# Hybrid encoder trunk: activations kept as [channels, tokens] from the first stage to the output

## Chip, cores and metric

One core of one Trainium2 chip. The metric is the device time of one launch in microseconds: the kernel before took 3477.07 us (median of 3 runs, 3474.01 to 3480.54).

## What is computed

Two groups of tokens (2048 and 256, together T = 2304) pass through two layers with shared weights, D = 1024. Every float32 operand of a large product is held as two parts, hi and lo, in TensorE's one-pass format (fp32r), and a product is three matmuls (`mm3`).

```python
# layer 0
h = x + concat(gqa(rms(x)), diff_attention(rms(x))) @ w_out_ab      # 8 rotary heads, 4 differential heads
h = h + sigmoid(rms(h) @ w_ple_gate[0]) * (p[0] @ w_ple_proj[0])
# layer 1
u, g = split(rms(h) @ w_in_c)                                       # pooling mixer
h = h + ((pooled(u) - u) @ w_grp * scale * silu(g)) @ w_out_c
h = h + sigmoid(rms(h) @ w_ple_gate[1]) * (p[1] @ w_ple_proj[1])
```

## The kernel before

The program is one stream per engine, ordered by hand and by a scheduler. Its stages, with the place that each has in the profiled span:

1. **Stage 1** (0 to 295 us). For each of the 9 blocks of 256 tokens: x comes in as rows, two tiles of [128 tokens, 1024]; `norm_rows` (L181) takes the sum of squares on ACT, rsqrt and the scaling by row on POOL; `transpose_rows` (L189) turns each tile by 8 PE transposes (L195) into channels on the partitions and splits it from PSUM with ACT (hi, L117) and DVE (lo, L118). Then the rotary heads' projections. The split x also goes to DRAM (`xT_d`).
2. **Attention A and B with fillers** (295 to about 2350 us). `drive` interleaves the heads' steps with filler steps: `proj_b`, then `proj_out(0)`, `proj_ple(0)`, `fold_c`, `proj_ple(1)`, `proj_out(512)`. `proj_out` (L738) takes 128 tokens at a time: the activations (yh, yl) stand still and 512 columns of the weights move, 12 matmuls into one bank; DVE adds the residual (L756), which is loaded and stored as rows of `h_d`. `proj_ple` (L759) turns its input by two PE transposes (L768).
3. **Drain of proj_out(512)** and loading of the gate's weights (to 2424 us): 6 of the 8 weight chunks are loaded before, 2 after the drain.
4. **Gate of layer 0** (to 2631 us), 18 tiles of 128 tokens: `gate_half` (L875) twice a tile, 24 matmuls each with 512 weight columns moving (po, then pf), sigmoid on ACT (L883), product and sum on DVE (L884, L885); `turned` (L896) turns the next tile's normalised rows, 8 transposes among them.
5. **Pooling mixer** (to 3058 us), 9 blocks: here the weights stand still and 256 tokens move. The next block's x is turned (16 transposes) while the groups are multiplied.
6. **`out_ple`** (L945, to 3464 us), 18 tiles of 128 tokens: output projection of layer 1 (pa, weights moving, 48 matmuls of 512), norm, 8 transposes, gate (48 matmuls of 512), sum, store.

In stages 1, 4, 5 and 6 the rows that ACT and DVE split are read from PSUM. All DMAs go through SP's queue.

```python
def transpose_rows(xn, hi, lo, col):                      # L189
    for half in range(2):
        pt = pt_()
        for j in range(4):
            pe.transpose(pt[:, j * P : (j + 1) * P], xn[:, ...], ident)
        split_ps(pt..., hi[:, cs, col : col + P], lo[:, cs, col : col + P])
```

Of the kernel before, what the change touches and what calls it, by code (L numbers as in the profile page):

```python
# [33 lines left out]
WG_A = 6  # L34
# [5 lines left out]
def trunk_kernel(ctx: ExitStack, tc: tile.TileContext, ins, outs):  # L40
# [4 lines left out]
    pin = [ins["p_prompt"][:, 0], ins["p_sample"][:, 0]]  # L45
    yout = [outs[0][0], outs[1][0]]
# [24 lines left out]
    # activations between the stages; "h" and "l" are the two parts of a split value  # L71
# [7 lines left out]
    h_d = dscratch("h_d", [T, D])  # L79
    m_d = dscratch("m_d", [D, D])  # L80
    pp_d = [dscratch(f"pp{i}_d", [T, D]) for i in range(2)]

# [16 lines left out]
    # products that warm the array up while the first loads run  # L99
# [5 lines left out]
    def rstd_of(ss, scale, n, extra=None):  # L105
        """(ss * scale + eps) ** -0.5 on [P, n]"""
# [17 lines left out]
    def split_w(st, hi, lo, gain=None):  # L124
        """hi + lo = st (weights by rows) times gain by row"""
# [11 lines left out]
    def load_w(pool, w, rows_, cols, tag, gain=None, stage=None, most=512):  # L137
        """columns [(from, to), ...] of w, chunks of 128 rows: a list of split (hi, lo)"""
# [36 lines left out]
    def mm3(out, lhs, rhs, first, last):  # L175
        """out += (lhs_hi + lhs_lo).T @ (rhs_hi + rhs_lo), less lo * lo"""
# [4 lines left out]
    def norm_rows(pool, xt, nb=2):  # L181
        ss = small.tile([P, 1], F32, tag="ss", name="ss")
        xn = pool.tile([P, D], F32, tag="xn", name="xn", bufs=nb)
        ac.activation(xn, xt, AF.Square, accum_out=ss)  # L184
        r = rstd_of(ss, 1.0 / D, 1)
        po.tensor_scalar(out=xn, in0=xt, scalar1=r, scalar2=1.0, op0=ALU.mult, op1=ALU.mult)
        return xn
# [11 lines left out]
    def load_q(pool, row0, nh, t0, n):  # L199
        """the parts of q, each on both halves of the partitions: two [P, nh, n]"""  # L200
# [13 lines left out]
    # =========================== norm, projections of the rotary heads ===========================  # L214
    with tc.tile_pool(name="p1c", bufs=1, reuse_waits="tile") as p1c, \
# [10 lines left out]
        def chain(t0, xts):  # L226
            xh = p1.tile([P, KC, NB], F32R, tag="xh", name="xh")
            xl = p1.tile([P, KC, NB], F32R, tag="xl", name="xl")
            for tt, xt in enumerate(xts):
                transpose_rows(norm_rows(p1, xt, 1), xh, xl, tt * P)  # L230
            store2(xT_d, (xh, xl), lambda d: d[:, t0 : t0 + NB].rearrange("(c p) t -> p c t", p=P))
# [506 lines left out]
    def proj_out(k0):  # L738
# [3 lines left out]
        for tq in TILES[k0 // 512]:  # L742
            while not ready[k0 // 512][tq // P]:
                yield 0.0
# [388 lines left out]
```

## Time and profile before

| | |
|---|---|
| median of 3 runs | 3477.07 us |
| span of the profiled execution | 3470.0 us |
| the median less that span | 7.07 us |
| TensorE matmul busy | 3408.2 us, 98% of the span |
| weight load, DVE, ACT, POOL busy | 88%, 56%, 48%, 48% |
| chain that ended last | PE 91%, DMA 4%, DVE 2%, ACT 1%, issue 1% |
| DMA | 437.76 MB, mean 126 GB/s |

The last matmul ends at about 3465 us; behind it are a sigmoid, two DVE operations and the last store. A matmul's record is longer than its turn on the array, since matmuls are pipelined: its price is the distance from one start to the next.

### The profile page before, as it was taken

The page shows a single profiled execution, that of the slowest core. Times are in us where ns is not written, and L with a number is a line of the kernel's source. Part 1 is how long each engine was busy: PE and PEld are TensorE (multiplying, and loading weights), DVE is VectorE, ACT ScalarE, POOL GpSimd, SP SyncE. Part 2 cuts the span into 40 slices and gives each one's busy share as a digit, 9 for nine tenths or more (in the row PEclk, how much of TensorE's full clock was granted, in tenths as well). Part 3 has the DMA queues.
Part 4 walks back from the last instruction along what each step waited for, and adds up shares of the span by engine and source line. Part 5 has one row for each costly group of instructions (what it writes and reads, how often), then busy time and mean ns, then how long its engine had stood idle before and what let it go on. Part 6 is the DMA issues. An engine that isn't in the chain of part 4 may idle for free.

```text
span 3470.0 us, 60660 instructions
## 1 busy us (share of the span) xinstructions
PE 3408.2 (98%) x21942; PEld 3043.7 (88%) x21942; DVE 1936.7 (56%) x4314; ACT 1671.8 (48%) x3108; POOL 1662.0 (48%) x2013
## 2 busy tenths in 40 slices
PE   9999999999999999999999899999999999999999
PEld 8998999998899988888888788887889999988887
DVE  4336666677666677658778787763434222342222
ACT  4235666666666666546677676751324111221111
POOL 5664545454645455337777687841113455420000
PEclk9999999999999999999999999999999999999999
DMA  7444323234423224653443525268534122353332
GB/s 250 158 141 135 112 77 109 79 109 125 141 82 98 91 77 127 190 180 108 122 125 114 149 91 149 87 196 267 186 133 157 62 72 70 99 164 115 112 113 73
DMA packets 459635, 437.76 MB, mean 126 GB/s; under 512 B 33992, under 2 KB 400584, under 8 KB 458312
## 3 DMA queue, kind: packets, MB, share of 16 engines
q1 hardware_dynamic: 459336, 433.88, 40.4%
q8 instruction: 174, 2.85, 0.3%
q14 instruction: 125, 1.02, 0.1%
HBM read 269.15 MB, written 164.63 MB: 125 GB/s over the span
## 4 chain that ended last, share of the span: by engine, by line
PE 91%; DMA 4%; DVE 2%; ACT 1%; issue 1%; POOL 0%; SPq 0%; DVEq 0%; ACTq 0%; POOLq 0%
PE pf L177 10%; PE pf L179 10%; PE pf L178 10%; PE pt L339 9%; PE pa L377 6%; PE pa L378 6%; PE po L177 6%; PE po L179 6%; PE po L178 6%; PE pa L178 4%; PE pa L177 4%; PE pa L179 4%; PE po L471 3%; PE po L470 3%; PE pt L195 2%; DMA v<-vl_d 1%
## 5 line engine op out<-in xcount | busy, mean ns | idle before, releaser
L389 ACT ACTIVATE s<-s,mx 128x1024 f32<-128x1024 f32 x512 | 585.6, 1147 | 137.3 <-DVE s L442 63.4
L347 DVE TENSOR_TENSOR pl<-pt,ph 128x512 fp32r<-128x512 f32 x780 | 522.4, 686 | 195.0 <-ACT ph L343 188.1
L343 ACT CAST ph<-pt 128x512 fp32r<-128x512 f32 x780 | 438.7, 584 | 276.3 <-PE pt L339 113.5
L339 PE MATMUL pt<-ident,s 128*128 128x128 f32 x3120 | 465.3, 273 | 4.5 <-DVE pl L347 1.9
L339 PEld LDWEIGHTS pt<-ident,s 128*128 128x128 f32 x3120 | 369.7, 141 | 52.4 <-DVE pl L347 4.6
L109 POOL TENSOR_SCALAR rstd<-ss 128x1 f32<-128x1 f32 x72 | 16.0, 222 | 656.4 <-ACT xn L184 654.8
L623 DVE CUSTOM_DVE_ANT_0 s<-pa,dist,mx 128x512 f32<-128x512 f32 x384 | 286.7, 747 | 70.5 <-PE pa L378 55.8
L643 POOL TENSOR_TENSOR s<-s 128x1024 f32<-128x1024 f32 (+1 forms) x136 | 313.0, 2318 | 0.2
L452 POOL TENSOR_SCALAR s<-s,rs 128x1024 f32<-128x1024 f32 (+1 forms) x272 | 298.6, 1110 | 12.1
L442 DVE TENSOR_SCALAR_CACHE_REDUCE s<-pa,mx 128x512 f32<-128x512 f32 x384 | 286.0, 745 | 23.2 <-PE pa L378 13.9
L470 PE MATMUL po<-ph,vA 128*128 128x256 f32 x1040 | 281.2, 292 | 1.1 <-ACT ph L343 1.1
L471 PE MATMUL po<-pl,vA 128*128 128x256 f32 x1040 | 279.5, 295 | 1.1 <-DVE pl L347 1.1
L177 PE MATMUL pf<-xh,wh 128*128 128x256 f32 x944 | 265.6, 281 | 1.7 <-DMA xh<-xTh_d 1.7
L178 PE MATMUL pf<-xl,wh 128*128 128x256 f32 x944 | 266.3, 282 | 0.5 <-DMA xl<-xTl_d 0.5
L179 PE MATMUL pf<-xh,wl 128*128 128x256 f32 x944 | 265.8, 282 | 0.7 <-DVE wl L131 0.7
L377 PE MATMUL pa<-kk,q 128*128 128x512 f32 (+1 forms) x528 | 220.8, 419 | 12.8 <-DMA kk<-kTl_d 11.5
L377 PE MATMUL pa<-kA,q 128*128 128x512 f32 (+1 forms) x528 | 222.8, 422 | 3.9 <-DVE s L442 3.7
L884 DVE TENSOR_TENSOR sg<-pp,sg 128x512 f32<-128x512 f32 x72 | 50.3, 698 | 285.3 <-ACT sg L883 280.0
L378 PE MATMUL pa<-kA,q 128*128 128x512 f32 (+1 forms) x528 | 207.0, 392 | 0.0
L378 PE MATMUL pa<-kk,q 128*128 128x512 f32 (+1 forms) x528 | 206.9, 392 | 0.0
L470 PEld LDWEIGHTS po<-ph,vA 128*128 128x128 f32 x1040 | 196.8, 189 | 11.3 <-ACT ph L343 1.7
L471 PEld LDWEIGHTS po<-pl,vA 128*128 128x128 f32 x1040 | 196.7, 189 | 7.5 <-DVE pl L347 3.0
(232 smaller groups left out, 9701.0 us busy)
## 6 DMA issues: line engine op xcount, KB each, us to landing
xr<-h_d SPq DMA_DIRECT2D x54, 512.0 KB, 3.3
q<-qTh_d SPq DMA_DIRECT2D x144, 128.0 KB, 2.9
q<-qTl_d SPq DMA_DIRECT2D x144, 128.0 KB, 3.0
xh<-xTh_d SPq DMA_DIRECT2D x18, 1024.0 KB, 5.5
xl<-xTl_d SPq DMA_DIRECT2D x18, 1024.0 KB, 7.9
h_d<-xr SPq DMA_DIRECT2D x72, 256.0 KB, 4.0
pp_d<-xr SPq DMA_DIRECT2D x72, 256.0 KB, 2.1
pp<-pp_d SPq DMA_DIRECT2D x36, 512.0 KB, 3.8
```

Of the source, the lines that this page charges most:

```text
L177: pe.matmul(out, lhsT=lhs[0], rhs=rhs[0], start=first, stop=False)
L178: pe.matmul(out, lhsT=lhs[0], rhs=rhs[1], start=False, stop=False)
L179: pe.matmul(out, lhsT=lhs[1], rhs=rhs[0], start=False, stop=last)
L339: pe.transpose(pt[:, (c * 2 + i) * P : (c * 2 + i + 1) * P], s[:, (c0 + c) * P : (c0 + c + 1) * P], ident)
L343: ac.copy(ph, pt)
L347: ve.tensor_tensor(out=pl, in0=pt, in1=ph.bitcast(F32), op=ALU.subtract)
L377: pe.matmul(ps, lhsT=q1, rhs=k[:, i * 512 : i * 512 + w], start=True, stop=False)
L378: pe.matmul(ps, lhsT=q2, rhs=k[:, i * 512 : i * 512 + w], start=False, stop=True)
L389: ac.activation(s[:, c], s[:, c], AF.Exp, bias=bias, scale=-1.0, accum_out=sums[i])
L470: pe.matmul(ov[0][:, 0:256], lhsT=v, rhs=ph[:, c], start=c0 + c == 0, stop=False)
L471: pe.matmul(ov[0][:, 0:256], lhsT=v, rhs=pl[:, c], start=False, stop=c0 + c == nk - 1)
L643: po.tensor_tensor(out=sc[0][:, k], in0=sc[0][:, k], in1=sc[1][:, k], op=ALU.subtract)
```

## The change

Host side: `xT` [1024, 2304] and `pT` are handed to the kernel beside the rest, and the outputs come back as [1024, tokens].

On the chip:

- The residual lives as `hT_d` [D, T] (two of them), the embedding's projection as `pp_d` [D, T]. A block is 256 tokens with all 1024 channels, tile [128, 8, 256], loaded in pieces of 1 KB.
- Normalising is `scaled`: r of 256 tokens is spread over the partitions by two PE transposes, ACT copies it (L190), and POOL multiplies the block by it in two instructions of 128x1024 (L192; in the mixer DVE does this). `split_sb` then splits in SBUF: ACT casts (L196), DVE subtracts (L197), 1024 columns each, twice.
- The sums of squares need PE too: ACT squares, POOL or DVE adds, and `tok_sums` multiplies by a column of ones (L204, 4 matmuls of one column, float32, per block).
- In the gates, `out_c`, `proj_out` and `proj_ple` weights stand still and 256 tokens move: each matmul of 512 columns becomes two of 256.
- Gate 0 finds r of the next block from a load of h (`r_here`) while it works on this one; the mixer and gate 1 use r kept from sums of the stage before (`r_all`). The gate's last sum moves from DVE to POOL (L1033).
- All 8 chunks of gate 0's weights are loaded before the drain ends, and the first block's chain starts among `proj_out(512)`'s last blocks.
- `proj_out` fetches y and the residual one step ahead; its buffers for the residual go from 4 to 3.
- The last stage is two passes over the blocks: `out_c` for all 9 (h stored), then gate 1.
- In stage 1 the first block is still turned by 16 transposes; the other eight use `scaled`.

```diff
+    def scaled(ht, r, xn, rb, eng=po):
+        pr = pt_()
+        for i in range(2):
+            pe.transpose(pr[:, i * P : (i + 1) * P], r[:, i : i + 1].broadcast_to([P, P]), ident)
+        ac.copy(rb, pr[:, :NB])
+        for cs in HALVES:
+            eng.tensor_tensor(out=xn[:, cs], in0=ht[:, cs], in1=rb.unsqueeze(1).broadcast_to([P, KC // 2, NB]), op=ALU.mult)
+
+    def split_sb(xn, hi, lo):
+        for cs in HALVES:
+            ac.copy(hi[:, cs], xn[:, cs])
+            ve.tensor_tensor(out=lo[:, cs], in0=xn[:, cs], in1=hi[:, cs].bitcast(F32), op=ALU.subtract)
+
+    def tok_sums(sm, n):
+        pst = pt_()
+        for i in range(2):
+            for k in range(n):
+                pe.matmul(pst[:, i : i + 1], lhsT=sm[:, k, i * P : (i + 1) * P], rhs=ones[:, 0:1], start=k == 0, stop=k == n - 1)
+        return pst[:, 0:2]
...
     def proj_out(k0):
...
-                xr = fw.tile([P, 512], F32, tag="xr", name="xr", bufs=4)
+            xr = fw.tile([P, 2, NB], F32, tag="xr", name="xr", bufs=3)
...
-                    mm3(ps, (yh[:, c], yl[:, c]), W[a // 128 + c], c == 0, c == 3)
+                        mm3(ps[:, m * NB : (m + 1) * NB], (w[0][:, ms], w[1][:, ms]), (yh[:, c], yl[:, c]), c == 0, c == 3)
...
+    def product(W, x, j):
+        ps = (po_, pf_)[j % 2]()
+        for m in range(2):
+            ms = slice((j * 2 + m) * P, (j * 2 + m + 1) * P)
+            for c in range(KC):
+                mm3(ps[:, m * NB : (m + 1) * NB], (W[c][0][:, ms], W[c][1][:, ms]), (x[0][:, c], x[1][:, c]), c == 0, c == KC - 1)
+        return ps.rearrange("p (m t) -> p m t", t=NB)
...
+        def chain(t0):
+            ht = h_block(src, t0)
+            xn = pool.tile([P, KC, NB], F32, tag="sq", name="xn", bufs=1)
+            r = yield from r_of(t0, ht, xn)
+            scaled(ht, r, xn, work[0].tile([P, NB], F32, tag="rb", name="rb"))
+            x = parts()
+            split_sb(xn, *x)
+            return ht, x
...
+            for j in range(KC // 2):
+                js = slice(j * 2, j * 2 + 2)
+                ps = product(W, x, j)
+                now, pp = pp, embedded(b * 4 + j + 1)
+                if j == 0 and pend:
+                    pend.pop()()
+                sg = pool.tile([P, 2, NB], F32, tag="sg", name="sg", bufs=2)
+                ac.activation(sg, ps, AF.Sigmoid)
+                ve.tensor_tensor(out=sg, in0=now, in1=sg, op=ALU.mult)
+                po.tensor_tensor(out=ht[:, js], in0=ht[:, js], in1=sg, op=ALU.add)
+                sy.dma_start(dst(t0)[:, js], ht[:, js])
+                if more:
+                    summed(pool, acc, ht[:, js], j)
+                if j < 3:
+                    go()
...
+    def r_here(t0, ht, sq):
+        sm = pw.tile([P, 2, NB], F32, tag="sm", name="sm", bufs=1)
+        for i, cs in enumerate(HALVES):
+            ac.activation(sq[:, cs], ht[:, cs], AF.Square)
+            ve.tensor_reduce(out=sm[:, i], in_=sq[:, cs].rearrange("p c t -> p t c"), axis=AX.X, op=ALU.add)
...
-    WG0 = load_w(pw, wpg[: WG_A * P], WG_A * P, [(0, D)], "wg", gple[0][:, :WG_A])
+    WG0 = load_w(pw, ins["w_ple_gate"][0], D, [(0, D)], "wg", gple[0])
+    while not through:
+        next(fill)
+    chain = gate_chain(pw, hT_d[0], r_here)
+    first = run(chain(0))
     for _ in fill:
         pass
...
-    out_ple("right", ins["w_out_c"][0], 0, ycT_d, 1, lambda t: rows(yout, t, P))
...
+            for j in range(KC // 2):
+                js = slice(j * 2, j * 2 + 2)
+                ve.tensor_tensor(out=ht[:, js], in0=product(WO, y, j), in1=ht[:, js], op=ALU.add)
+                sy.dma_start(chans(hT_d[0], t0)[:, js], ht[:, js])
...
+        gate(pw, WG, 1, nxt, chain, lambda t0: chans(outs[0], t0) if t0 < S0 else chans(outs[1], t0 - S0), None, iter(()))
```

Counted over the program: 3888 matmuls of 512 columns become 7776 of 256 (gates 1728, `out_c` 864, `proj_out` 864, `proj_ple` 432); of the 576 transposes at L195, 16 stay, so 70 groups of 8 go; the 36 pairs at L768 go; 35 pairs of transposes for r and 27 groups of 4 one-column matmuls come.

What the change moves, at two places. First TensorE in gate 0. Before, a tile's last matmuls into po and the next tile's transposes, which are followed by this tile's pf:

```order
L177 MATMUL po<-wh,nh 128x512
L178 MATMUL po<-wl,nh 128x512
L179 MATMUL po<-wh,nl 128x512
L195 MATMUL pt<-ident,xn 128x128 x8
L177 MATMUL pf<-wh,nh 128x512
L178 MATMUL pf<-wl,nh 128x512
```

Now, in the last group (pf) of a block, the two transposes that spread the next block's r (rt):

```order
L175 MATMUL pf<-yh,wh 128x256
L176 MATMUL pf<-yl,wh 128x256
L177 MATMUL pf<-yh,wl 128x256
L189 MATMUL pt<-ident,rt 128x128 x2
L175 MATMUL pf<-yh,wh 128x256
L176 MATMUL pf<-yl,wh 128x256
```

Before, a whole group of 24 matmuls of 512 stood between the transposes and the products that need them; now 30 matmuls of 256 follow the r transposes in every other block, and 46 in the blocks between, before the next block's first product.

Second, POOL in gate 0 (rstd, rt, r_all: the factors r; xn: the normalised tile; ht: the residual; acc: the squares' sum). Before, one tile after the other:

```order
L109 TENSOR_SCALAR rstd<-ss 128x1
L112 TENSOR_TENSOR rstd<-rstd,mhalf 128x1
L186 TENSOR_SCALAR xn<-xr,rstd 128x1024
L109 TENSOR_SCALAR rstd<-ss 128x1
L112 TENSOR_TENSOR rstd<-rstd,mhalf 128x1
```

Now, one block:

```order
L210 TENSOR_TENSOR r_all<-r_all,mhalf 128x2
L1033 TENSOR_TENSOR ht<-ht,sg 128x512
L1054 TENSOR_TENSOR acc<-acc,sq 128x512
L210 TENSOR_TENSOR rt<-rt,mhalf 128x2
L1033 TENSOR_TENSOR ht<-ht,sg 128x512
L192 TENSOR_TENSOR xn<-ht,rb 128x1024 x2
L1054 TENSOR_TENSOR acc<-acc,sq 128x512
```

The scaling was one instruction with one tensor operand for 128 tokens, done long before its turn; it is two instructions with two tensor operands for 256 tokens, between the sums of the block that is being worked on, and it stands behind the r transposes.

## Rows read from the trace of the kernel before

**Rows 1.** The page: busy time of each engine; shares of the chain that ended last

```profile
PE 3408.2 (98%) x21942; PEld 3043.7 (88%) x21942; DVE 1936.7 (56%) x4314; ACT 1671.8 (48%) x3108; POOL 1662.0 (48%) x2013
PE 91%; DMA 4%; DVE 2%; ACT 1%; issue 1%; POOL 0%; SPq 0%; DVEq 0%; ACTq 0%; POOLq 0%
```

**Rows 2.** Timeline of PE (start, duration, line, out<-in, shapes, count), mixer, first and last of 17

```profile
2799.76 0.28 PE L177 MATMUL po<-xh,wh 128*128 128x256 f32 x1
...
2801.64 0.28 PE L178 MATMUL pf<-xl,wh 128*128 128x256 f32 x1
```

**Rows 3.** Timeline of PE, one tile of out_ple

```profile
3199.82 0.40 PE L178 MATMUL pa<-wl,yh 128*128 128x512 f32 x1
3204.96 0.39 PE L179 MATMUL pa<-wh,yl 128*128 128x512 f32 x1
3205.19 1.04 PE L195 MATMUL pt<-ident,xn 128*128 128x128 f32 x8
3205.98 0.48 PE L177 MATMUL pa<-wh,yh 128*128 128x512 f32 x1
3206.30 0.40 PE L178 MATMUL pa<-wl,yh 128*128 128x512 f32 x1
3211.67 0.40 PE L177 MATMUL po<-wh,nh 128*128 128x512 f32 x1
3222.35 0.40 PE L179 MATMUL pf<-wh,nl 128*128 128x512 f32 x1
```

**Rows 4.** Timeline of PE in stage 1, first and last of 19 matmuls

```profile
259.76 0.28 PE L177 MATMUL pf<-xh,wh 128*128 128x256 f32 x1
...
261.92 0.28 PE L177 MATMUL pf<-xh,wh 128*128 128x256 f32 x1
```

**Rows 5.** Groups by line, PE: shapes, count, busy us, mean ns of one, idle before

```profile
L195 PE MATMUL pt<-ident,xn 128*128 128x128 f32 x576 | 76.7, 273 | 2.3 <-POOL xn L186 2.3
L768 PE MATMUL pf<-ident,pl 128*128 128x128 f32 x72 | 14.1, 273 | 0.1
```

**Rows 6.** Timeline of PE, one-column matmuls (each leaves two records)

```profile
2342.77 0.50 PE L673 MATMUL pt<-ones,sq 128*128 128x1 f32 x4
2343.13 0.48 PE L178 MATMUL pa<-wlo,yh 128*128 128x512 f32 x1
2343.45 0.39 PE L179 MATMUL pa<-whi,yl 128*128 128x512 f32 x1
```

**Rows 7.** Timeline of PE, transposes that spread a row's factor

```profile
1906.70 0.38 PE L681 MATMUL pt<-ident,rstd 128*128 128x128 f32 x2
1906.91 1.47 PE L339 MATMUL pt<-ident,s 128*128 128x128 f32 x12
```

**Rows 8.** Lines of ACT, DVE and POOL: instructions nearest to the added ones

```profile
L184 ACT ACTIVATE xn<-xr 128x1024 f32<-128x1024 f32 x50 | 53.5, 1070 | 96.0 <-issue 80.0 <-DVE xr L974 16.1
L885 DVE TENSOR_TENSOR xr<-xr,sg 128x512 f32<-128x512 f32 x72 | 49.6, 689 | 3.0
L643 POOL TENSOR_TENSOR s<-s 128x1024 f32<-128x1024 f32 x128 | 307.2, 2417 | 0.0
```

**Rows 9.** Timeline of POOL, then of DVE, in attention B

```profile
1577.62 4.76 POOL L643 TENSOR_TENSOR s<-s 128x1024 f32<-128x1024 f32 x2
...
1580.74 2.19 DVE L128 TENSOR_TENSOR wlo<-st,whi 128x512 fp32r<-128x512 f32 x1
1584.12 0.68 DVE L128 TENSOR_TENSOR wlo<-st,whi 128x512 fp32r<-128x512 f32 x1
```

**Rows 10.** Timeline of PE: waits in the drain and at gate 0's start

```profile
2337.38 0.47 PE L177 MATMUL pa<-whi,yh 128*128 128x512 f32 x1 [2.32 <-DVE xr L756]
...
2420.63 0.50 PE L177 MATMUL po<-wh,nh 128*128 128x512 f32 x1 [1.90 <-ACT wh L130]
2426.87 0.50 PE L177 MATMUL po<-wh,nh 128*128 128x512 f32 x1 [1.86 <-ACT sg L883]
```

**Rows 11.** Windows, PE, after the first of these waits

```profile
2338.00:2342.00 4.00, 4.00 (x12) 0.60 0.94 320
```

More of the change, by code (lines that the diff above doesn't have):

```diff
@@ new lines, in parts, with gate_chain @@
+    def parts():
+        pool = turn(1)
+        return [pool.tile([P, KC, NB], F32R, tag=t, name=t) for t in ("yh", "yl")]
+    def gate_chain(pool, src, r_of):
+        def chain(t0):
[6 more added lines that the diff above has]
+            return ht, x
+        return chain
@@ new lines, in paired, with go, value, keep_r @@
+    def paired(step):
+        got = []
+        def go():
+            if not got:
+                try:
+                    next(step)
+                except StopIteration as e:
+                    got.append(e.value)
+        def value():
+            while not got:
+                go()
+            return got[0]
+        return go, value
+    def keep_r(pend, acc, t0):
+        pend.append(lambda: rstd_ps(tok_sums(acc, 2), r_all[:, t0 // P : t0 // P + 2]))
+    def gate(pool, W, layer, nxt, chain, dst, more, after):
+        def embedded(n):
+            if n < len(BLOCKS) * 4:
+                pp = pool.tile([P, 2, NB], F32, tag="pp", name="pp", bufs=2)
+                sy.dma_start(pp, chans(pp_d[layer], BLOCKS[n // 4])[:, n % 4 * 2 : n % 4 * 2 + 2])
+                return pp
+        pend, pp = [], embedded(0)
+        for b, t0 in enumerate(BLOCKS):
+            ht, x = nxt
+            go, value = paired(chain(t0 + NB) if t0 + NB < T else after)
+            go()
+            if more:
+                acc = pool.tile([P, 2, NB], F32, tag="acc", name="acc", bufs=1)
+            for j in range(KC // 2):
+                js = slice(j * 2, j * 2 + 2)
[8 more added lines that the diff above has]
+                sy.dma_start(dst(t0)[:, js], ht[:, js])
+                if more:
+                    summed(pool, acc, ht[:, js], j)
+                if j < 3:
+                    go()
+            nxt = value()
+            if more:
+                keep_r(pend, acc, t0)
+                more(t0)
+        while pend:
+            pend.pop()()
+        return nxt
@@ L946, in trunk_kernel, with mid, chain_c @@
-    transpose_rows(xn, *x0, P)
+    def mid(t0):
+        if t0 == 2 * NB:
+            load_c(wp[0], 0)
+    def chain_c(t0, late=0):
+        ht = h_block(hT_d[1], t0)
+        for _ in range(late):
+            yield
+        scaled(ht, r_all[:, t0 // P : t0 // P + 2], ht, work[0].tile([P, NB], F32, tag="rb", name="rb"), ve)
+        x = parts()
+        split_sb(ht, *x)
+        return x
+    nxt = gate(gx, WG0, 0, first, chain, lambda t0: chans(hT_d[1], t0), mid, chain_c(0, 2))
     for p_ in ple0[::-1]:
@@ L993, in trunk_kernel, with loaded @@
+    def loaded(t0):
+        y = parts()
+        load2(ycT_d, y, lambda d: chans(d, t0))
+        return y, h_block(hT_d[1], t0)
     with pool_ as ws:
```

301 lines of the change are left out of this document (151 added, 150 removed).

## Prediction

> **What bounds the kernel now.** The page comes first: TensorE is busy for 98% of the span, and the chain that ended last is PE for 91% [rows 1]. So the time is the sum of what each matmul takes of the array, plus the moments in which TensorE waits. Busy time is of no use for the first (records overlap), so I read the timelines for the distance from start to start [rows 2 to 4, 6, 7], and for the second the bracketed waits of the same view [rows 10]. The reader is to see how even the starts are: a matmul with 512 moving columns comes every 0.227 us in the gate (47 steps from 3211.67 to 3222.35) and every 0.2336 us in `out_c` (22 steps from 3199.82 to 3204.96) [rows 3]; one with 256 columns comes every 0.1175 us in the mixer (16 steps) [rows 2] and every 0.120 us in stage 1 (18 steps) [rows 4]. Neither half is half of the whole.
>
> **Terms on TensorE.**
> - *512 columns become twice 256.* I take 0.1185 us for 256, between the two rows that I have, since no row tells which of them the new stages resemble. A gate pair then costs 0.237 against 0.227: 1728 x 0.010 = +17. `out_c`: 864 x 0.0034 = +3. The fillers have the gate's shape and I give them 8 ns each: 1296 x 0.008 = +10. Sum +30. By 0.1175 it is 7776 x 0.001 = 8 less, by 0.120 it is 12 more.
> - *Transposes that go.* Eight take 0.79 us (3205.19 to 3205.98), and the matmul behind them takes 0.32 instead of 0.23 [rows 3]: 0.88 a group. 70 of the 72 groups behind the 576 records go [rows 5]: -62. The 36 pairs on the embedding go [rows 5], each 0.21 [rows 7] and some re-entry: -8.
> - *What comes.* 35 pairs for r at the same 0.23: +8. One group of `tok_sums` is four one-column matmuls; two of them (four records) take 0.36, and the next matmul 0.09 more than usual [rows 6]: 0.72 + 0.09 = 0.81, times 27 = +22.
>
> Together 30 - 70 + 30 = **-10 us**, between -18 and +2. The gain from no longer turning is mostly spent on the halves and the sums.
>
> The Trainium skill has another price for the halves: "TensorE: Matmul & The Clock Gate", section "Back-to-back issue gap", gives N columns over 2.4 GHz plus about 2.5 ns. By that estimate two halves cost only 2.5 ns more than the whole, +10 instead of +30. The starts of [rows 2 to 4] do not agree with it, so the sum does not use it.
>
> **Terms in waits.** Before, the next tile's turning was a whole group ahead. Now the next block's chain starts at the r transposes. I price it in gate 0, from the transposes on: the pair 0.3; the copy of 256 columns, a quarter of a 1.07 us ACT row, 0.3 [rows 8]; POOL's two products, 2.42 each by the nearest two-operand row of that size; ACT's cast of 1024 columns, 1.07; DVE's subtraction, two rows of 0.69, 1.3 [rows 8].
>
> The subtraction now reads two tensors in SBUF, where before it read PSUM and SBUF. Beside a busy POOL that means this: a DVE subtraction of two SBUF operands takes 0.68 alone, but 2.19 when it starts at 1580.74 while POOL's second product of a pair runs [rows 9]. POOL ends at 1582.38 and DVE at 1582.93, 0.55 later. It did not slow down, it stood until POOL was through. So the first half's lo cannot be made while POOL makes the second half.
>
> Thus, counted from the transposes: first POOL product to 3.0; cast to 4.2 (hi is there); second POOL product to 5.5; DVE to 6.8 (lo of the first half); cast of the second half to 6.6, DVE to 8.1. TensorE has 30 matmuls to go in half of the blocks (3.9 us with the pair) and 46 in the others (5.8). The next block's first product needs hi at once, lo one matmul later, and the second half 12 matmuls later, 1.4 us. In the short case it waits 6.8 - 3.9 = 2.9, in the long one 1.0. Four blocks of each: **+16 us**. Bounds: if DVE is not held, the second half still ends near 7.9 and the sum is about 10; if a further two-operand DVE instruction of the block (0.69) catches POOL in each half, it is 27.
>
> The other places:
> - *Gate 0's first block.* Its chain has only 24 matmuls of the drain to hide under (2.8 us): some 4 us of waiting. It replaces the waits of 1.90 and 1.86 that stand at the same place now [rows 10]: 0.
> - *Head of stage 1.* The second block's chain, the same 8 us, starts behind ACT's and DVE's splitting of the weights: +4, between 0 and 8.
> - *Start of the mixer.* DVE scales and splits there while it also makes the lo parts of the mixer's weights (two SBUF operands), beside POOL's pooling: +4, between 0 and 8.
> - *`proj_out`.* Fetching ahead would take away waits for the residual like the 2.32 in rows 10, but with three buffers the load of a step waits for the store of three steps earlier: 0, between -5 and +8.
> - *Last stage.* Its chain runs a whole block ahead (192 matmuls, 23 us), its 19 MB more of DMA (h of 2304 x 1024 float32 stored and loaded once more) are spread over 400 us, and the mixer's and gate 1's r is kept: 0. If that cover went, it would cost the 8 us of the chain per block.
> - Fewer instructions on POOL, ACT and DVE in the turned stages: 0, those engines end no chain there.
>
> **Sum.** -10 + 16 + 0 + 4 + 4 + 0 = +14 us. The profiled execution's span of 3470.0 becomes 3484; the median stands 7.07 above that span, so I forecast **3491 us**.
>
> **Rivals.**
> 1. *The chain is covered: faster.* Place: the start of each gate block. It decides whether POOL's two products and what follows end before pf's last matmuls; the point is a chain of about 5.5 us instead of 8.1, that is POOL products of 1.1 us, or a scheduler's 46 matmuls that turn out longer than the chain's first half. Then the 16 us and the two 4s fall away, and the TensorE term stands alone: 3477 - 10 = 3467. For it: POOL's queue has little else in gate 0, and the mixer's turned chain left no waits. Against it: the 2.42 us rows, 128 of them. 0.13.
> 2. *Half of the waits: no change.* The hold of DVE costs less because DVE's queue is in step with POOL, head and mixer cost nothing: -10 + 10 = 0, 3477. 0.20.
> 3. *Cheap halves.* The new matmuls come at 0.1137, half of 0.2275, if a matmul's turn has next to no fixed part, so that two halves cost a whole: the +30 falls to +10 and the forecast to 3471. No row shows such a pace. This is what the Trainium skill's issue gap, cited above, amounts to. 0.05.
> 4. *Slower still.* A wait above two microseconds can also cost the clock: after the wait of 2.32 the granted clock was 0.60 over 4 us, a mix of 1.2 and 2.4 GHz, with 12 matmuls where 17 fit, 1.2 us lost [rows 10, 11]; behind the waits of 1.90 and 1.86 no such loss is seen. Were all four long waits to trip it and POOL be caught by DVE as in the upper bound: 3491 + 11 + 5 = 3507. 0.12.
>
> That the change does not take the turning away is excluded: the transposes are gone from the order.
>
> **How the numbers follow.** The forecast has the remaining 0.50. About 0.2%, 7 us, is what a measurement of this kernel can tell from none, so "faster" is under 3470 and "slower" over 3484. Faster: rival 1 for the most part, and a little of rivals 2 and 3: 0.13. The same: most of rivals 2 and 3, and a little of the forecast's lower end: 0.25. Slower: 0.62. The range leaves out the far halves of rivals 1 and 4: 3467 to 3508. The forecast's own range, from its bounds, is 3480 to 3503.
>
> **What would show it.** Right: no L195 in the mixer and the last stage; starts 0.237 apart per pair in the gates; in gate 0, waits of 1 to 3 us at each block's first product, with DVE's subtraction (L197) as releaser; L197's mean well over 1.3 us there; the stage longer than before, the mixer and stage 1 shorter by 5 to 10 us each. Wrong: no waits at gate 0's blocks; pairs at 0.227; or waits of `out_c` and gate 1 on loads, which I priced at nothing.

## The result, and the profile after

The changed kernel takes 3529.89 us (median of 4 runs, 3529.05 to 3542.31), the kernel before 3476.5 beside it: ratio 1.0161, 95% interval [1.0146, 1.0176]. It is slower, as forecast, but by 53 us and not by 14: outside the range of 3467 to 3508.

The profiled execution of that run was a long one (span 3540.5). The same kernel was profiled again in the first experiment (span 3525.9, run's median 3526.94), and the rows below are of that execution unless another is named. First the page: busy time of TensorE, and the shares of the chain that ended last, to be laid beside [rows 1].

```profile
PE 3425.6 (97%) x25484; PEld 3225.4 (91%) x25484; DVE 2024.4 (57%) x4199; ACT 1684.4 (48%) x3037; POOL 1929.0 (55%) x2042
PE 81%; DMA 6%; DVE 5%; issue 3%; POOL 3%; ACT 1%; SPq 0%; POOLq 0%; DVEq 0%; ACTq 0%
```

The share of TensorE in the chain falls from 91% to 81%; DMA, DVE, POOL and issue, 7% together before, are now 17%. TensorE is busy at almost the same share: the page's first line alone would hide the change.

A table by stage says where. Each border is the start of a matmul in the timeline: the first that reads kA, the last that reads v, the last on the fillers' weights (whi, wlo), the last on gate 0's weights, the last on the mixer's, the last of all. Lengths in us:

| | stage 1 | attention | drain | gate 0 | mixer | last stage | last matmul starts |
|---|---|---|---|---|---|---|---|
| before | 292.2 | 2041.4 | 82.0 | 210.0 | 424.6 | 414.4 | 3464.6 |
| changed | 288.9 | 2049.8 | 90.6 | 259.4 | 413.6 | 417.6 | 3519.9 |
| difference | -3.3 | +8.4 | +8.6 | **+49.4** | -11.0 | +3.2 | +55.3 |
| by the terms of the prediction | -8 | +2 | 0 | +25 | -10 | +5 | +14 |

The mixer and the last stage came as forecast. Nearly all the loss is in gate 0, 6% of the span before. Its waits on TensorE (who waits, who ends the wait, us in total, times, longest), from 2440 to 2700 us:

```profile
PE po L176 <- DVE yl L197: 13.4, 11, 2.4
PE pt L204 <- DVE sm L1060: 6.1, 9, 1.5
PE po L175 <- ACT yh L196: 4.8, 5, 2.1
PE pt L189 <- POOL rt L210: 0.3, 1, 0.3
```

In gate 0 of the kernel before, TensorE waits 3.8 us, the two waits of 1.90 and 1.86 in [rows 10]. The second line is one that the prediction has no word for: the one-column matmuls of `tok_sums` wait for the sums that DVE makes.

Windows of the same stage, of before and then of the changed kernel (length, TensorE busy and matmuls, weight loads, DVE, ACT, POOL, granted clock, DMA share, GB/s):

```profile
2500.00:2550.00 50.00, 50.00 (x242) 41.85 (x241) 15.78 (x25) 13.74 (x26) 7.46 (x12) 1.00 0.42 142
2550.00:2600.00 50.00, 50.00 (x238) 41.77 (x237) 17.73 (x28) 14.55 (x28) 8.41 (x15) 1.00 0.41 137
```

```profile
2440.00:2500.00 60.00, 51.96 (x406) 50.35 (x404) 30.51 (x31) 22.01 (x36) 35.10 (x23) 0.94 0.46 144
2500.00:2550.00 50.00, 44.39 (x345) 42.63 (x346) 21.18 (x18) 14.93 (x22) 32.02 (x20) 0.97 0.31 96
2550.00:2600.00 50.00, 46.03 (x380) 44.87 (x379) 18.35 (x17) 14.91 (x23) 25.98 (x19) 1.00 0.38 117
2600.00:2650.00 50.00, 44.48 (x350) 42.86 (x348) 22.08 (x18) 15.88 (x22) 26.62 (x17) 0.97 0.34 106
2650.00:2700.00 50.00, 47.92 (x371) 47.33 (x372) 18.71 (x24) 18.07 (x30) 26.86 (x19) 0.93 0.42 130
```

Two things are to be seen. TensorE is no longer full (44 to 48 of 50), and the granted clock is under 1.00 in four of five windows. A window's clock is a mean over stretches at 2.4 GHz and others at 1.2; what is missing to 1.00, times the window, is the work that was lost, or a little more, since a wait inside a slow stretch is counted too: 0.06 x 60 + 0.03 x 50 + 0 + 0.03 x 50 + 0.07 x 50 = 10.1 us. So of the +49 in gate 0, 21 are waits (24.6 - 3.8), up to 10 are clock, and the remaining 18 are matmuls (9 were forecast; e7 below, almost without waits, gives about 13) and the slow restarts behind each wait: the matmul after the one at 2513.66 below starts 0.23 us later, where the next ones come every 0.113.

Gate 0 is not the only place where the clock fell. Over the whole span the mean granted clock is 0.991, and 0.998 before; the same product gives 32 us against 7. Of these 25 us more, 10 are in gate 0, the others in stage 1, the drain and the attention.

Now one block, in the timelines of ACT, DVE, POOL and TensorE (start, duration; in brackets the idle time before and what ended it). This is the chain that the prediction costed:

```profile
2497.40 2.01 ACT L1059 ACTIVATE xn<-ht 128x1024 f32<-128x1024 f32 x2 [4.33 <-DMA ht<-hT_d]
2506.95 0.37 ACT L190 COPY rb<-pt 128x256 f32<-128x256 f32 x1
2510.16 1.05 ACT L196 CAST yh<-xn 128x1024 fp32r<-128x1024 f32 x1 [2.85 <-POOL xn L192]
2512.56 1.05 ACT L196 CAST yh<-xn 128x1024 fp32r<-128x1024 f32 x1 [1.35 <-POOL xn L192]
...
2498.49 3.82 DVE L1060 TENSOR_REDUCE sm<-xn 128x256 f32<-128x1024 f32 x2 [4.57 <-ACT xn L1059]
2511.24 4.59 DVE L197 TENSOR_TENSOR yl<-xn,yh 128x1024 fp32r<-128x1024 f32 x2 [3.42 <-ACT yh L196]
...
2507.39 5.14 POOL L192 TENSOR_TENSOR xn<-ht,rb 128x1024 f32<-128x1024 f32 x2 [1.08 <-ACT rb L190]
2512.49 2.27 POOL L1033 TENSOR_TENSOR ht<-ht,sg 128x512 f32<-128x512 f32 x1
...
2500.50 0.38 PE L204 MATMUL pt<-ones,sm 128*128 128x1 f32 x2 [1.42 <-DVE sm L1060]
2506.49 0.38 PE L189 MATMUL pt<-ident,rt 128*128 128x128 f32 x2
2513.66 0.38 PE L176 MATMUL po<-yl,wh 128*128 128x256 f32 x1 [1.17 <-DVE yl L197]
2513.89 0.28 PE L177 MATMUL po<-yh,wl 128*128 128x256 f32 x1
2515.89 0.39 PE L176 MATMUL po<-yl,wh 128*128 128x256 f32 x1 [0.60 <-DVE yl L197]
```

Read from the top. ACT stands 4.33 us for the load of ht, squares it, DVE reduces (two strided reductions, 3.82), and TensorE has to stop for them at 2500.50, in the middle of the block before. From the r transposes at 2506.49 the rest goes as worked out, a little slower: POOL's products end 6.0 later (5.5 forecast), lo of the first half is there after 7.2 (6.8), lo of the second after 9.4 (8.1). DVE's two subtractions take 2.3 each in place of 1.3; POOL works on SBUF tensors through the first 3.5 of their 4.6 us, first the product, then the sum L1033, which itself takes 2.27 here and 1.29 elsewhere in the block.

### The profile page after: what moved, and what is told of

Read it like the earlier page. It is cut to its first block, busy times and chain, and to the rows that moved or that the text cites. A ratio compares the mean times of both kernels' runs of the same rounds, so it can differ in the third digit from the quotient of the medians.

```text
span 3540.5 us, 67631 instructions
## 1 busy us (share of the span) xinstructions
PE 3431.6 (97%) x25484; PEld 3230.8 (91%) x25484; DVE 2017.3 (57%) x4199; ACT 1686.7 (48%) x3037; POOL 1925.8 (54%) x2042
## 4 chain that ended last, share of the span: by engine, by line
PE 79%; DMA 8%; DVE 4%; issue 3%; POOL 3%; ACT 2%; SPq 1%; POOLq 0%; DVEq 0%; ACTq 0%
PE pf L175 10%; PE pf L176 10%; PE pf L177 10%; PE pt L377 9%; PE pa L415 6%; PE po L176 6%; PE po L177 6%; PE pa L416 6%; PE po L175 6%; PE po L509 3%; PE po L508 3%; DMA hT_d<-xr 1%; DMA xt<-in_x_prompt_dram 1%; PE pa L175 1%; PE pa L176 1%
## 5 line engine op out<-in xcount | busy, mean ns | idle before, releaser
L176 PE MATMUL po<-yl,wh 128*128 128x256 f32 x1440 | 408.7, 284 | 16.8 <-DVE yl L197 16.8
L175 PE MATMUL po<-yh,wh 128*128 128x256 f32 x1440 | 407.8, 283 | 7.0 <-ACT yh L196 6.1
L175 PE MATMUL pf<-yh,wh 128*128 128x256 f32 x1440 | 408.1, 283 | 1.4 <-ACT z L1161 0.9
L177 PE MATMUL pf<-yh,wl 128*128 128x256 f32 x1440 | 406.3, 282 | 2.7 <-DVE wl L129 2.7
L177 PE MATMUL po<-yh,wl 128*128 128x256 f32 x1440 | 407.0, 283 | 0.8 <-DVE wl L129 0.8
L176 PE MATMUL pf<-yl,wh 128*128 128x256 f32 x1440 | 405.9, 282 | 0.0
L176 PEld LDWEIGHTS po<-yl,wh 128*128 128x128 f32 x1440 | 276.6, 192 | 19.4 <-DVE yl L197 19.4
L175 PEld LDWEIGHTS po<-yh,wh 128*128 128x128 f32 x1440 | 276.0, 192 | 8.4 <-ACT yh L196 7.3
L175 PEld LDWEIGHTS pf<-yh,wh 128*128 128x128 f32 x1440 | 275.2, 191 | 2.7 <-ACT z L1161 1.3
L177 PEld LDWEIGHTS po<-yh,wl 128*128 128x128 f32 x1440 | 276.3, 192 | 1.2 <-DVE wl L129 1.2
```

Source lines behind the costliest of these rows:

```text
L175: pe.matmul(out, lhsT=lhs[0], rhs=rhs[0], start=first, stop=False)
L176: pe.matmul(out, lhsT=lhs[0], rhs=rhs[1], start=False, stop=False)
L177: pe.matmul(out, lhsT=lhs[1], rhs=rhs[0], start=False, stop=last)
```

## The experiments

**Theory A:** gate 0's chain comes too late for TensorE (late load, slow sums, POOL's products with DVE held beside them), each short wait costs restart and clock too, and the matmuls as such cost little. **Theory B:** the 256-column halves, the added sums and pairs are what costs. Each kernel ran beside the kernel before (3474.8 to 3475.6 us in these runs).

The scheduler makes the order of every engine's stream, so an edit can also move instructions that it does not name. In the traces, e10 has the changed kernel's order of TensorE in the drain and gate 0; the other edited kernels do not, not even e4, whose edit is in stage 1 alone. A gain of one edit is therefore that of the edit with its new order.

| | edit | median us | ratio to before [95%] | gate 0 | drain |
|---|---|---|---|---|---|
| e1 | none | 3526.94 | 1.0145 [1.0130, 1.0160] | 259.4 | 90.6 |
| e2 | sums by adds | 3517.28 | 1.0123 [1.0106, 1.0140] | 251.6 | 89.0 |
| e3 | third h buffer, one step earlier | 3505.50 | 1.0082 [1.0067, 1.0098] | 235.5 | 89.2 |
| e4 | stage 1 turned | 3526.58 | 1.0145 [1.0130, 1.0160] | 252.3 | 88.5 |
| e5 | e3 + e2 | 3503.61 | 1.0079 [1.0063, 1.0096] | 235.5 | 89.4 |
| e6 | products on DVE | 3514.30 | 1.0107 [1.0092, 1.0122] | 244.3 | 91.3 |
| e7 | e3 + e2 + e6 | 3489.28 | 1.0040 [1.0029, 1.0052] | 226.4 | 89.2 |
| e8 | e7, first block early | 3488.61 | 1.0035 [1.0022, 1.0048] | 224.9 | 89.4 |
| e9 | changed + idle matmuls | 3532.59 | 1.0166 [1.0148, 1.0183] | 261.5 | 92.0 |
| e10 | changed, moved 64 bytes | 3523.10 | 1.0135 [1.0117, 1.0153] | 257.8 | 92.4 |
| e11 | e8, moved 192 bytes | 3481.18 | 1.0009 [0.9996, 1.0023] | 222.1 | 91.2 |
| e12 | e11, two blocks turned | 3467.64 | **0.9975** [0.9963, 0.9988] | 217.7 | 86.5 |

**e1, the changed kernel again.**

> The changed kernel once more, as the base of this call and for a second trace. Both theories: 3527 to 3533 us. The first trace's execution was 13 us longer than the others, with a granted clock of 0.86 to 0.97 in many stretches of 50 us; if those stretches are chance, this trace has fewer of them at the places of attention B, while the waits in gate 0 (about 37 us more than before) stand as they were.

Measured 3526.94, at the lower edge: the difference is there again, and the table of stages above is this run's.

**e2, the strided reductions become two adds of contiguous tiles.**

```diff
-            ve.tensor_reduce(out=sm[:, i], in_=sq[:, cs].rearrange("p c t -> p t c"), axis=AX.X, op=ALU.add)
+        ve.tensor_tensor(out=sq[:, 0:4], in0=sq[:, 0:4], in1=sq[:, 4:8], op=ALU.add)
+        ve.tensor_tensor(out=sm, in0=sq[:, 0:2], in1=sq[:, 2:4], op=ALU.add)
```

> In gate 0 the two strided DVE reductions of the squares (1.95 us each in the trace) become two additions (1.23 and 0.69 expected). Theory A (gate 0 loses its time to the chain that makes the next block's normalised halves, and that chain starts too late): the waits for sm at the one-column matmuls (10 us in all) fall under 3 us, and the kernel to about 3520 (3514 to 3525). Theory B (the loss is in the 256-column matmuls themselves, the waits only take up slack): no change, 3527 to 3533.

Measured 3517.28, 9.7 us less, as A said. TensorE's waits for the sums in gate 0 fall from 6.1 to 0.7. A reduction took 1.97 us in the mean, two a block; the adds took 1.22 and 0.69. But the order on TensorE changed too: the r transposes now stand 33 matmuls ahead of the next block in six of eight blocks, not 30 and 46 by turns. And e4 below has these waits at 1.5 by another order alone, with drain and gate 0 together 9.2 us shorter than in e1; in e2 they are 9.4 shorter. So the wait for the sums is real, but e2 does not show what the reductions alone cost.

**e3, a third buffer for the block of h, and its chain one step earlier.**

```diff
+        if third:
+            ring = work + third
+            blocks_[0] += 1
+            pool = ring[(blocks_[0] - 1) % 3]
...
         r = rstd_ps(tok_sums(sm, 2), small.tile([P, 2], F32, tag="rt", name="rt"))
-        yield
         return r
...
+    third.append(gx)
```

> A third buffer for h in gate 0, and one pause less in its chain, so that a block's load need not wait for the stores of two blocks before; nothing else. The r transposes then stand 51 matmuls before the next block in every block instead of 30 and 46. Theory A: the waits for sm go (10 us), those for yh and yl fall from 21 to about 10, the clock loss behind them (7 us) halves: 3500 to 3512. Theory B: 3527 to 3533.

Measured 3505.50, 21 us less, the largest single step, and no product is different, only the order. With two buffers the load of a block cannot start before the block two earlier is stored, and this lateness goes through squares, sums and r to the products. SP, which issues all loads, stood for that store in front of the load (L969) nine times in e1, once a block:

```profile
SPq L969 <- DMA hT_d<-ht: 17.1, 9, 2.4
```

In e1 the squares at 2497.40 start 14.6 us after their block's first product. In e3 the block that starts at 2508.49 has them, without a wait for the load, 2.9 us after it:

```profile
2511.36 2.01 ACT L1067 ACTIVATE xn<-ht 128x1024 f32<-128x1024 f32 x2
```

The earlier step puts the r transposes 52 or 53 matmuls ahead of the next block, in place of 30 and 46. Buffer and step were not run apart. From 2500 to 2650 the granted clock is 1.00 again. All waits in gate 0 fall from 24.6 to 12.3, most of what is left being those for yl:

```profile
PE po L176 <- DVE yl L197: 9.7, 15, 2.8
```

Gate 0 is 23.9 us shorter, so about half of this gain is waits, the rest clock and restarts. Theory B cannot give it.

**e4, all blocks of stage 1 turned on TensorE as before.**

```diff
-            if t0:
+            if t0 > 10 ** 6:
```

> Stage 1 alone as before: all nine blocks turned by PE (128 transposes back, 8 pairs for r gone). Theory A: TensorE has 12 us more to do, and the waits at the head (12 us, 6 of them before the second block's first product) go down to the 4 us of the kernel before: 3528 to 3536, no change in all. Theory B: the same sums without the waits' part: 3540 to 3544.

Measured 3526.58, just under A's range and far from B's. Stage 1 is 5.3 us longer than in the changed kernel though its waits are shorter: the waits of the head, below, are the part of the change's gain that is eaten there. The attention is 5.0 us longer and drain and gate 0 are 9.2 shorter, none of which the edit touches, so that no change in all is in part luck. Gate 0's waits here, to be laid beside those above:

```profile
PE po L176 <- DVE yl L197: 12.8, 12, 1.5
PE po L175 <- ACT yh L196: 7.5, 4, 5.4
PE pt L204 <- DVE sm L1060: 1.5, 4, 0.4
```

In the changed kernel, TensorE's waits in the first 295 us were

```profile
PE pt L219 <- POOL xc L267: 4.0, 2, 2.5
PE pa L175 <- ACT xh L196: 2.5, 1, 2.5
PE pa L177 <- DVE xl L197: 1.7, 1, 1.7
```

The last two are the second block's, 4.2 us, just the 4 that were forecast; with a granted clock of 0.91 between 20 and 60 us (3.6 us lost, before 1.00) the stage gained 3.3 instead of 8.

**e5, e6, e7: both edits, the products alone, all three.** The edit of e6, in the chain that gates 0 and 1 share, so that it holds for both:

```diff
-            scaled(ht, r, xn, work[0].tile([P, NB], F32, tag="rb", name="rb"))
+            scaled(ht, r, xn, work[0].tile([P, NB], F32, tag="rb", name="rb"), ve)
```

> The changed kernel with a third buffer for the gate's h block and the sum of squares by two adds instead of two strided reductions (the two edits that alone gave 3505.5 and 3517.3 against 3526.9). Theory A (gate 0 loses time because its chain starts late and each of its waits sets the clock back): both edits shorten the same chain, so they add up only in part; the buffer took 21 us, the adds alone 10, of which the waits for sm were already gone with the third buffer in gate 0 but not in its first block, where 4 us of them are left: 3498 to 3503. Theory B (the 256-column halves are what costs): both edits touch no matmul, so what is left over the kernel before stays near 30 us and the two together give no more than the buffer alone, 3505 or above.

> The changed kernel with one word more: gate 0's two products h*r by VectorE in place of POOL, nothing else. Theory A says that L197's wait-makers are POOL's two products (2.55 us each) and the hold of VectorE by POOL while they run (L197 takes 2.15 in the mean, 1.21 at least); on VectorE a product took 1.46 us, so the chain from rb to the last yl is shorter by 2 to 4 us a block and the waits for yl in gate 0 (13.4 us of 20) fall by half or more, with some of the half-clock stretches behind them: 3508 to 3518. If POOL's hold does not matter and only the late start does (buffers), VectorE's longer row of work gives the gain back: 3523 to 3530.

> Third h buffer, adds and products on VectorE together. Theory A: almost no wait is left in gate 0 outside its first block, the clock there is 1.00, and gate 0 takes 210 (before) plus about 9 of matmul work, 217 to 224 in place of 259: 3488 to 3496. What then stays over the kernel before (12 to 20 us) is the first block's wait (6 to 9) and the halves and pairs in attention (about 8). Theory B: 3505 or above as for the buffer alone.

e5 measured 3503.61, between A's range and B's, and no better than e3 within the intervals: once the chain starts early, the sums are off the path, and the 4 us that were to come from the first block did not (e8 shows why). By itself e5 does not tell the theories apart. e6 measured 3514.30, 12.6 us less, in A's range, but not all in A's way: the waits for yl, which were to fall by half, fell from 13.4 to 12.1 in all. From the fourth block on, those for yh and yl are 1.0 to 1.3 us a block instead of 1.7 to 2.2; the second and third, in another order, wait longer. DVE's subtractions in the two gates, of the changed kernel and of e6 (count, busy, mean ns of one):

```profile
L197 DVE TENSOR_TENSOR yl<-xn,yh 128x1024 fp32r<-128x1024 f32 x36 | 77.4, 2150 | 42.9 <-ACT yh L196 42.5
```

```profile
L197 DVE TENSOR_TENSOR yl<-xn,yh 128x1024 fp32r<-128x1024 f32 x36 | 45.8, 1280 | 0.1
```

The same 36 instructions on the same tiles, half of them in gate 0: 2.15 us beside POOL's products, 1.28 when the products come ahead of them on DVE itself; in gate 0 alone 1.95 and 1.34. POOL did these products in 2.55 us each, DVE in 1.55. The Trainium skill, "SBUF — State Buffer", section "Who interferes with whom", says that a DVE instruction with two inputs in SBUF contends with a GpSimd instruction that reads SBUF. The rows agree, 2150 against 1280 ns.

e7 measured 3489.28, in the lower part of A's range and far from B's 3505. Three windows of gate 0 in e7, against the same ones above:

```profile
2440.00:2500.00 60.00, 55.97 (x453) 55.47 (x452) 28.39 (x33) 22.78 (x37) 26.37 (x21) 0.94 0.52 162
2500.00:2550.00 50.00, 50.00 (x425) 50.00 (x425) 24.93 (x24) 18.58 (x26) 23.46 (x18) 1.00 0.41 127
2550.00:2600.00 50.00, 50.00 (x426) 50.00 (x425) 24.95 (x24) 18.63 (x27) 23.43 (x18) 1.00 0.41 127
```

425 matmuls fit where 345 and 380 had been, and TensorE is full from 2500 on. Gate 0 takes 226, 16 more than before and a little more than the 217 to 224 expected. Its waits, 4.0 us, are no longer than before (3.8); the clock of the first window gives 0.06 x 60 = 3.6, and about 13 are left for the matmuls.

**e8, the first block ahead of the gate's weights.**

```diff
-    WG0 = load_w(pw, ins["w_ple_gate"][0], D, [(0, D)], "wg", gple[0])
     while not through:
         next(fill)
     chain = gate_chain(pw, hT_d[0], r_here)
-    first = run(chain(0))
+    c0 = chain(0)
+    next(c0)
+    WG0 = load_w(pw, ins["w_ple_gate"][0], D, [(0, D)], "wg", gple[0])
+    first = run(c0)
```

> The three edits, and the first block of gate 0 started ahead of the gate's weights: its h load is issued before the 16 weight transfers on SP's queue, and its squares and sums stand ahead of the weights' splits on ACT and VectorE. The stretch of the drain holds 8.6 us more than before, of which 6.3 are waits for sm and yl in that first block. If the place in the queues is the cause, 4 to 8 us come off: 3482 to 3491. If not (the last tiles of the fill write the h block too late for anything to start earlier), no change against the three edits.

Measured 3488.61: no change against e7. TensorE's waits in the drain (2345 to 2440), of the changed kernel and of e8:

```profile
PE pt L204 <- DVE sm L1060: 4.7, 2, 2.9
PE po L176 <- DVE yl L197: 2.9, 1, 2.9
PE po L175 <- ACT yh L196: 1.1, 1, 1.1
```

```profile
PE pa L175 <- DMA yh<-yTh_d: 6.4, 1, 6.4
PE pa L175 <- DVE xr L821: 4.2, 4, 2.2
PE po L175 <- ACT yh L196: 2.8, 1, 2.8
```

The names have changed and the sum has grown (8.7, 13.4). e7 has the same three waits already (5.2, 5.6 and 2.8), so this edit added nothing. When TensorE no longer stops for the first block's sums, it comes sooner to the last blocks of `proj_out`, whose activations and residuals are not there yet: a wait that takes the place of the one removed. Why that load is so late was not tried.

**e9, work for TensorE in front of each wait.** 16 matmuls on weights, overwritten by the block's first product.

```diff
+                if j == 0 and b and more:
+                    busy = po_()
+                    for i in range(16):
+                        pe.matmul(busy[:, :NB], lhsT=W[0][0][:, 0:P], rhs=W[i % KC][0][:, 0:NB], start=True, stop=True)
```

> The changed kernel, with 16 more matmuls of 256 columns (on weights alone, their result is overwritten) ahead of each block of gate 0 but the first, in the place where TensorE waits for yh and yl. They are 8 blocks x 16 x 0.12 = 15.4 us of work that nobody needs. If the waits cost only their length, the work fills waits (13.4 us for yl and 4.8 for yh in that stretch) and the time stays within 4 us of the changed kernel's 3527. If the half clock behind the waits is a cost of its own (20 us in that stretch by the trace), it goes with them, and the kernel with more work is faster: 3508 to 3520, with a granted clock of 0.98 to 1.00 in gate 0. If the waits there are none that work can fill, it is 15 us slower: 3540 and above.

Measured 3532.59, between the first expectation (3531 at most) and the last (3540 and above), far from the second, and not apart from 3526.94 by the intervals. In gate 0 the waits for yl fell from 13.4 to 4.2, for yh from 4.8 to 0.6, but those for the sums rose from 6.1 to 9.7, presumably since the sums' chain does not move with the block. The granted clock was 0.94, 0.93, 1.00, 1.00, 1.00 in the five windows: 0.06 x 60 + 0.07 x 50 = 7.1 us lost, where the changed kernel lost 10. So 15 us of idle work cost 2 us in the stage, and clock is a part of what a wait costs, but the larger part is the lateness itself. The 20 us of half clock in the expectation were too high: they are the length of the slow stretches, and at half clock only half of it, the 10 us above, is lost.

**e10 and e11, addresses.** In the mixer of the changed kernel something shows that has nothing to do with waits. Windows in five consecutive blocks, all of them full and at clock 1.00:

```profile
2750.00:2780.00 30.00, 30.00 (x267) 30.00 (x266) 9.71 (x19) 3.94 (x7) 14.01 (x19) 1.00 0.25 84
2795.00:2825.00 30.00, 30.00 (x253) 30.00 (x252) 8.84 (x17) 3.93 (x7) 13.39 (x17) 1.00 0.23 78
2840.00:2870.00 30.00, 30.00 (x267) 30.00 (x267) 9.08 (x17) 3.94 (x7) 15.21 (x19) 1.00 0.26 88
2886.00:2916.00 30.00, 30.00 (x253) 30.00 (x252) 7.95 (x16) 3.93 (x7) 14.59 (x18) 1.00 0.18 62
```

267 and 253 matmuls by turns. A window also counts the matmuls that its ends cut; from start to start they come every 0.113 and 0.120 us. The blocks alternate between two buffers for yh and yl. Their addresses leave 224 and 32 over a multiple of 256, the weights' 32. The two kernels move tiles by unused ones:

```diff
     work.append(ctx.enter_context(tc.tile_pool(name="work1", bufs=1, reuse_waits="tile")))
+    work[1].tile([P, 48], F32, tag="pad0", name="pad")
...
     WG0 = load_w(pw, ins["w_ple_gate"][0], D, [(0, D)], "wg", gple[0])
+    pw.tile([P, 48], F32, tag="pad", name="pad")
```

(16 words instead of 48 in e10; in both, one more of 16 words behind the buffer's tiles. In e10 the mixer's weights move by 128 bytes with them, to a remainder of 160, and the two buffers stand at 96 and 224; in e11 both stand at 224 and the weights at 32.)

> The changed kernel with three unused tiles of 64 bytes a partition, which move activations against weights: in gate 0, the mixer and the last stage, each moving tile begins 96 bytes behind a multiple of 128, each weight tile 32. In the trace of the changed kernel the slot of a 256-column matmul fell in classes by these two remainders: 119 to 120 ns where both are alike, 118 at 32 (moving) and 96, 113.4 at 96 and 32, which is half of the mixer's. If the remainders are the cause, all 8640 matmuls of the three stages come to 113 to 114 ns: gate 0 1728 x 5.5 = 9 us (some of it taken back as longer waits), mixer 3456 x 3.7 = 13, last stage 3456 x 4 = 14, so 3490 to 3503 in place of 3527. If it is something else that goes with the two buffers (what is in the blocks, or what runs beside them), no change: 3522 to 3532. By the theory that the halves themselves are dear, their price has a part that an address sets.

> The kernel of e8 with unused tiles (192 and 64 bytes in the pool of the second ring buffer, 192 behind gate 0's weights), which put every moving tile of gate 0, the mixer and the last stage at 224 and every weight tile at 32, counted from a multiple of 256. The move by 64 bytes gave 4 us of 24 to 37, and its trace fits another rule: by the difference, moving less stationary, in units of 256 bytes, the slot of a 256-column matmul was 120 ns at 0, 118 at 64 and 113.4 at 192, and the move had turned one buffer from 0 into 192 and the other from 192 into 64. By that rule all 8640 slots come to 113.4 to 115: gate 0 1728 x 5 = 9, mixer 3456 x 3.5 = 12, last stage 3456 x 3 = 10, 24 to 31 us of which gate 0 may give some back in waits: 3458 to 3470 in place of 3488.6, faster than the kernel before. If the address has no such rule: 3483 to 3493.

e10 measured 3523.10, 4 us less, which the intervals do not tell from none: the rule of the remainders of 128 fell. But the blocks did change. The first two of the same windows in e10, then in e11:

```profile
2750.00:2780.00 30.00, 30.00 (x257) 30.00 (x256) 9.29 (x19) 3.93 (x7) 10.46 (x15) 1.00 0.27 88
2795.00:2825.00 30.00, 30.00 (x267) 30.00 (x266) 9.83 (x18) 3.94 (x7) 15.02 (x18) 1.00 0.27 88
```

```profile
2750.00:2780.00 30.00, 30.00 (x267) 30.00 (x266) 12.61 (x19) 5.83 (x9) 17.17 (x18) 1.00 0.23 77
2795.00:2825.00 30.00, 30.00 (x267) 30.00 (x267) 12.65 (x19) 5.83 (x9) 17.78 (x19) 1.00 0.24 81
```

In e11 the blocks of the mixer run at 267 per 30 us, and the mixer takes 402.9 in place of 413.8. There the rule held. It did not in the last stage (257 per 30 us, 417.2 us as without the move) nor fully in gate 0 (222.1 against 224.9 in e8); in these two stages the weight tiles are four times as wide as in the mixer. So e11's 3481.18 is 7 us under e8 where at least 18 were expected. That the place of a tile sets a matmul's pace is shown; the rule for it is open.

**e12, two blocks of stage 1 turned.**

```diff
-            if t0:
+            if t0 > NB:
```

> The kernel of e11 with the first two blocks of stage 1 turned by TensorE as the kernel before does, in place of the first alone. TensorE waited 6.1 us in one piece at 40.7 us for the second block's xh, behind the weights' loads and splits; turning it costs the transposes (8 x 2 of 0.1 us and more, and the evictions) but not the wait for the second x transfer. With all four later blocks turned, stage 1 took 5.3 us more and waited 4 less, so a block's turn costs about 2.5 us net of waits: 1 to 4 us faster than e11 if the wait goes, 2 us slower if it moves on to the third block.

Measured 3467.64, 13.5 less than e11, where 1 to 4 were expected. Stage 1 gives 4.8 of it: the waits for the second block's xh and xl (4.5 us in e11) are gone from its list, with only 1.6 us of others in their place. The drain and gate 0 are 4.7 and 4.4 us shorter too, in stages that the edit does not touch. TensorE's order is another there: 68 of gate 0's matmuls stand ahead of the last one on the fillers' weights, in e11 17, while from gate 0's second block to its end both take the same (198.6 in e11, 198.7). The waits from 2345 to 2440, of e11 and of e12:

```profile
PE pa L175 <- DMA yh<-yTh_d: 5.9, 1, 5.9
PE pa L175 <- DVE xr L821: 4.4, 3, 3.6
PE po L175 <- ACT yh L196: 2.8, 1, 2.8
```

```profile
PE pa L175 <- DVE xr L821: 7.1, 2, 6.2
```

So this part of the gain is one of order, not of the edit as such. e11's own runs spread from 3467 to 3484, with a granted clock of 0.994 and 0.995 in the two shortest and of 0.990 to 0.993 in the others, so the step between the two is less sure than the last comparison: e12 is faster than the kernel before, 0.9975 [0.9963, 0.9988]. The moved tiles are part of that, and they might be worth as much in the kernel before, where the mixer's 256-column matmuls come every 0.1175 us [rows 2]; this was not tried.

## Why the prediction was wrong in size

- **TensorE's term, -10: about right.** Mixer -11.0 (-10 forecast), last stage +3.2 (+5). The waits of `out_c` and gate 1 on loads, named as a sign of error, did not come.
- **Gate 0's waits, +16: right as far as they went.** For yh and yl TensorE waited 18.2 us (4.8 + 13.4), with L197 as the main releaser and a mean of 1.95 us in gate 0, as said under "What would show it". The hold of DVE by POOL [rows 9] was real (e6). The sum came nearer than its parts, which is luck: 4.5 us in the second block, then 2.2 and 1.7 by turns, where 2.9 and 1.0 were priced.
- **What failed first is a term that is missing: the sums.** The prediction costed `tok_sums` on TensorE (27 x 0.81) and left out the wait for their operand: two strided reductions of 1.97 us between the squares and L204. It was 6.1 us in gate 0 and 4.7 in the drain. With adds in place of the reductions, and the order that came with them, e2 is 9.7 us shorter; how much of this is the sums' alone is open, since e4 shows the wait fall to 1.5 by order. The chain was priced "from the transposes on", and the sums lie ahead of them.
- **What failed second is the start of the chain.** The r transposes were taken as given, at their place in the order, and there they stood. But everything ahead of them was late, because ht has two buffers and its load waits for the store of the block two before. e3 gives 21 us for one more buffer and an earlier step together, the largest share of the 53. For `proj_out` the prediction had reckoned with just this kind of wait, for gate 0 not.
- **Third, clock and restarts.** Rival 4 gave 5 us for the clock at 0.60 behind four long waits [rows 11] and a chance of 0.12 with all else. It was up to 10 us in gate 0 and 25 in the whole kernel; in gate 0 it stood behind waits that were mostly of 1 to 2 us but came in twos and threes a block. [rows 10] showed two waits of that length, 6 us apart, without such a loss: that was read as harmless, and many of them in a row were not.
- **Gate 0's first block, 0: +8.6 in the drain.** The 4 us expected for yh and yl are there (1.1 + 2.9), beside them the 4.7 for the sums, which had no term. The 3.8 at gate 0's start and 3.9 of the drain's own waits before are gone, and what remains is clock and restarts. e8's order does not get it back; e12's gets a part of it, with 7.1 us of waits there.
- **Halves in the fillers, +10, with -8 for the embedding's pairs: +8.4 for the attention.** There the halves came every 0.120 us (median; the whole, 0.227 to 0.231 before), so two cost about 11 ns more and not 8; by the means, 0.121 and 0.234, it is the 8. That is up to 4 of the 6 us that are missing. The rest is less than what the stage varies by: in none of the kernels here it was edited, and it took between 2042.8 (e8) and 2055.8 us (the first profile of the changed kernel).
- **Rival 3, "no row shows such a pace".** Half of the mixer's blocks show it, 0.113 against the 0.1137 which the rival needed, though in a stage whose matmuls had 256 columns before too. The Trainium skill, "TensorE: Matmul & The Clock Gate", section "Back-to-back issue gap", has a formula for an isolated matmul, which gives 109 ns for 256 columns, an estimate. e11's mixer, at 113, comes within 4% of it; gate 0, the fillers and the last stage, at 117 to 120, don't. The price of a half is not a constant of its shape.

## What to carry to other kernels

When a change makes a row of small steps a block's precondition, follow it back past the first instruction that you had in view: to the load, the buffer that the load waits for, and every reduction between. In a kernel whose matmul engine is full, a wait of 1 to 2 us that recurs each block can cost about twice its length, by restarts and clock (in e3, 23.9 us of gate 0 for 12.3 of waits); give such a chain its buffer and its head start before counting what the removed work saves. And two vector engines on SBUF operands at once can be slower than one alone doing both parts. Where a scheduler makes the order, compare the orders before a gain is put down to an edit: with e4's edit in stage 1, drain and gate 0 were 9.2 us shorter.

## What the runs showed of the hardware that was not expected

- The pace of a matmul of 256 columns with a weight load each depends on where its tiles lie: 0.113, 0.118 and 0.120 us from start to start (267, 257 and 253 in 30 us at clock 1.00), switched by moving tiles by 64 to 192 bytes. Over the mixer's 3456 matmuls this was 11 us.
- A strided reduction of 128x1024 to 128x256 on DVE took 1.97 us; an add of 1024 columns in one pass over contiguous tiles took 1.22 (e2), and 1.79 and 1.91 where it stood at another place in the order (e5, e7).
- A product of 128x1024 with two SBUF operands took 2.55 us on POOL (e1), and 1.31 and 1.55 on DVE (e7, e6).
